# Down-projection of a decoder layer: seven block products in place of eight, with weight sums made in an earlier stage

## The chip, the cores and the metric

One core of one Trainium2 chip runs the whole layer. The metric is device time in microseconds (us). Before the change the median of three runs is 3149.24 us (3142.88 to 3153.28); the execution that was profiled took 3145.07 us. Engines are named as in the profile: PE (TensorE), PEld (its weight loads), DVE (VectorE), ACT (ScalarE), POOL (GpSimd), SP (SyncE, which issues nearly all DMAs, in order).

## The reference

One layer over 2048 tokens of width 1024, all in float32: a normalised and modulated input projection, two kinds of causal attention (8 stick-breaking heads, then 8 "FoX" heads with forget gates), an output projection, a gated MLP with a width-3 causal convolution, and a last RMS norm. What the change touches is the end of it:

```python
h = rms_norm(x, g_mlp[l]) * (1.0 + scale_m) + shift_m
u = causal_depthwise_conv(h @ w_up[l], conv_w[l], conv_b[l])
u_gate, u_val = jnp.split(u, 2, axis=-1)
x = x + gate_m * ((jax.nn.silu(u_gate) * u_val) @ w_down[l])
return rms_norm(x, g_final)
```

`w_down` is 2752 x 1024, so the inner dimension is 21 full blocks of 128 channels and one of 64. `gate_m` is one number for each of the 1024 output columns, made from the conditioning vector `c`.

## The kernel before

**Precision.** A float32 product is made of three matmuls of a reduced-precision type. `split` (L43) writes the high part of an operand on ACT (`AF.Copy`, L44) and the remainder on POOL or DVE (`tensor_sub`, L45); the three matmuls are high x high, high x low, low x high. L44 and L45 are thus the lines of every operand in the profile; the tile's name tells which.

**Stages.** The stick-breaking attention takes the first 950 us or so, the FoX attention about 950 to 1640, the output projection to about 1790, the up-projection with convolution to about 2660, the down-projection to the end. In the attention stages `units` (L579) are (kind, head pair, block of 512 tokens); while one unit attends, `interleave` (L137) advances "fillers" by a number of steps for each unit: the next unit's projection (`proj`, L347, which loads eight `hp` tiles by L352), and, in the FoX stage, `late_mod` (L528). That generator makes the four later parts of the modulation from `w_ada` (ACT L554, POOL L552 and L555); after part 2 it folds the attention gate into `w_out` (`fold_out`, L515: 16 operand tiles stored to DRAM by L525), and after part 5 it stores the MLP's gate as `gate_m` (L568). It gets 4 steps for each unit from the second FoX unit on (L694). All its tiles are `hp` tiles (`h_tile`, L182, ten buffers of 512 KB), which the projection uses too. POOL has further work there: a memset for each diagonal tile of attention weights (L399), and small squares (L483).

**The up-projection** (L811 to L926) is already done as seven block products for eight (Winograd's form of Strassen's method): for each block of 128 channels POOL makes four sums of the weights (L799, L800, L801, L805), seven operands are split, and seven products run. Its results, `silu(u_gate) * u_val` with channels on the partitions, are stored to the DRAM tiles `gs` (L904, L926).

**The down-projection** (L929 to L996). For each of four blocks of 512 tokens, all 22 channel blocks are gone through. `load` brings 128 channels of `w_down` (512 KB, `wdraw`) and of `gs` (256 KB, `graw`) and splits both. 8 PSUM banks hold 4 token tiles x 2 column halves; each gets three matmuls of 128x128 by 128x512 for a channel block (two for the half block, whose two parts share one tile). At the end of a token block each bank is multiplied by the gate (`gm`, L986), added to the residual `xo` (L987), squared and normalised (L989 to L995), and written out.

**Order.** A list scheduler orders each engine's instructions when the program is built; every engine then runs its own list in order. A tile gets a buffer when one of its name's is free, so that a load into a buffer waits on SP for that buffer's last reader, and what stands behind it on SP waits too.

## Time and profile before

| what | us |
|---|---|
| median of three runs | 3149.24 |
| profiled execution | 3145.07 |
| its span on the core | 3143.3 |
| PE busy in the span | 2990.1 |
| DVE / ACT / POOL busy | 2158.8 / 1652.0 / 1215.3 |
| first matmul of the down-projection | 2662.12 |

A line of the groups view reads: line, engine, operation, tiles written and read, shape, count, then busy time and mean duration (ns) of one, then idle time of the engine ahead of them and who ended it. A row of the view by stretches gives, for a stretch of the span, the busy time and count of each engine, the granted clock of PE (1 is full), the share of the 16 DMA engines that was busy, and GB/s. A row of the timeline gives start, length, engine, line, operation and count. The view of waits gives who waited for whom, total us, times, longest.

### The profile page before, as it was taken

To read this page: it belongs to the slowest core of one execution; us is meant where nothing else is said; L and a number is where in the kernel's file an instruction comes from. 1 tells how busy PE (TensorE), PEld (TensorE's weight loads), DVE (VectorE), ACT (ScalarE), POOL (GpSimd) and SP (SyncE) were. 2 spreads that over 40 slices of the span, in tenths; PEclk is the share of its full clock that TensorE was granted. 3 is DMA by queue.
4 is the path that set the end of the run, shared out by engine and by line. 5 is a ranking of instruction groups with operands and counts; after the bars stand their busy time and mean duration, and the time that the engine had idled before them with its cause. 6 is when DMAs were issued, how large, how long until landed. Compare 5 with 4: busy or idle time off the path is not lost.

```text
span 3143.3 us, 46642 instructions
## 1 busy us (share of the span) xinstructions
PE 2990.1 (95%) x16190; PEld 2521.1 (80%) x16190; DVE 2158.8 (69%) x3343; ACT 1652.0 (53%) x3033; POOL 1215.3 (39%) x1391
## 2 busy tenths in 40 slices
PE   6899998999989999999999999999899998999998
PEld 5778787877878889888877678888678887888887
DVE  6787888978866775556843587777987776254253
ACT  5565666656756665556744444444444444343332
POOL 2563555647543132142112344444444442322321
PEclk8999999999999999999999999999999999999999
DMA  9447542455336695685546632222222223554552
GB/s 267 167 156 247 169 128 78 159 200 161 127 107 225 204 306 184 188 298 177 170 154 219 213 101 81 86 87 82 84 80 83 88 86 123 195 199 161 190 199 90
DMA packets 292941, 496.53 MB, mean 158 GB/s; under 512 B 29449, under 2 KB 177665, under 8 KB 291681
## 3 DMA queue, kind: packets, MB, share of 16 engines
q1 hardware_dynamic: 281072, 480.92, 47.9%
q10 hardware_dynamic: 11632, 12.63, 1.1%
q8 instruction: 128, 2.10, 0.3%
q14 instruction: 109, 0.88, 0.1%
HBM read 352.61 MB, written 90.51 MB: 141 GB/s over the span
## 4 chain that ended last, share of the span: by engine, by line
PE 57%; DVE 13%; DMA 12%; POOL 7%; issue 6%; ACT 4%; SPq 1%; ACTq 0%; POOLq 0%; DVEq 0%
PE ps_pj L287 8%; PE ps_o L963 8%; PE ps_pv L405 6%; PE ps_o L813 6%; PE ps_pt L396 5%; PE ps_pj L326 5%; PE ps_t L963 4%; PE ps_bc L963 4%; DMA wuraw<-in_w_up_dram 3%; PE ps_qk L384 3%; PE ps_qk L385 3%; DVE r L426 2%; DVE wu L45 2%; PE ps_t L813 2%; DMA Q<-q 2%
## 5 line engine op out<-in xcount | busy, mean ns | idle before, releaser
L813 PE MATMUL ps_o<-oa,wu 128*128 128x512 f32 x2088 | 503.3, 392 | 12.6 <-DVE oa L45 7.5
L813 PEld LDWEIGHTS ps_o<-oa,wu 128*128 128x128 f32 x2088 | 390.7, 188 | 104.2 <-DVE oa L45 11.8
L405 PE MATMUL ps_pv<-at,V 128*128 128x256 f32 x2304 | 416.4, 299 | 25.6 <-DVE at L401 12.5
L401 DVE TENSOR_TENSOR at<-ps_pt,at 128x512 fp32r<-128x512 f32 (+1 forms) x576 | 363.4, 651 | 109.1 <-ACT at L400 106.5
L400 ACT ACTIVATE at<-ps_pt 128x512 fp32r<-128x512 f32 (+1 forms) x576 | 315.7, 577 | 209.6 <-PE ps_pt L396 165.8
L287 PE MATMUL ps_pj<-hp,w_qk 128*128 128x512 f32 x1512 | 414.1, 405 | 11.9 <-POOL hp L45 3.4
L426 DVE TENSOR_TENSOR_SCAN r<-r 128x513 f32<-128x513 f32 (+2 forms) x320 | 383.6, 1213 | 40.2 <-ACT r L419 30.5
L427 POOL TENSOR_TENSOR a<-a,r 128x512 f32<-128x512 f32 (+3 forms) x240 | 280.3, 1171 | 310.5 <-DVE r L426 178.9
L405 PEld LDWEIGHTS ps_pv<-at,V 128*128 128x128 f32 x2304 | 339.0, 194 | 61.5 <-DVE at L401 25.1
L287 PEld LDWEIGHTS ps_pj<-hp,w_qk 128*128 128x128 f32 x1512 | 273.4, 190 | 65.8 <-POOL hp L45 4.5
L45 DVE TENSOR_TENSOR wd<-wdraw,wd 128x1024 fp32r<-128x1024 f32 x88 | 112.2, 1275 | 260.9 <-ACT wd L44 260.8
L384 PE MATMUL ps_qk<-K,Q 128*128 128x512 f32 (+2 forms) x640 | 269.5, 421 | 12.0 <-DMA K<-q 6.2
L45 POOL TENSOR_TENSOR g<-graw,g 128x512 fp32r<-128x512 f32 x84 | 141.4, 1685 | 325.9 <-ACT g L44 325.8
L963 PE MATMUL ps_o<-wd,g 128*128 128x512 f32 x1040 | 250.2, 390 | 8.8 <-ACT g L44 8.8
L326 PE MATMUL ps_pj<-w_v,hp 128*128 128x256 f32 (+1 forms) x1536 | 241.1, 293 | 3.8 <-DVE q L296 2.0
L813 PE MATMUL ps_t<-ob,wu 128*128 128x512 f32 x984 | 241.6, 390 | 0.0
L385 PE MATMUL ps_qk<-K,Q 128*128 128x512 f32 (+2 forms) x640 | 238.5, 373 | 0.0
L963 PEld LDWEIGHTS ps_o<-wd,g 128*128 128x128 f32 x1040 | 195.6, 188 | 49.8 <-ACT g L44 9.2
L44 ACT ACTIVATE wu<-wuraw 128x512 fp32r<-128x512 f32 x214 | 133.2, 626 | 184.4 <-PE ps_o L813 114.7
L326 PEld LDWEIGHTS ps_pj<-w_v,hp 128*128 128x128 f32 x1536 | 212.5, 194 | 13.3 <-DVE q L296 2.8
L813 PEld LDWEIGHTS ps_t<-ob,wu 128*128 128x128 f32 x984 | 184.8, 188 | 39.1 <-DVE wu L45 0.3
L396 PE MATMUL ps_pt<-ident,a 128*128 128x128 f32 x1088 | 185.6, 280 | 21.7 <-POOL a L427 13.2
(221 smaller groups left out, 5665.2 us busy)
## 6 DMA issues: line engine op xcount, KB each, us to landing
hp<-hs SPq DMA_DIRECT2D x224, 512.0 KB
wuraw<-in_w_up_dram SPq DMA_DIRECT2D x84, 512.0 KB
wdraw<-in_w_down_dram SPq DMA_DIRECT2D x84, 512.0 KB
Q<-q SPq DMA_DIRECT2D x128, 256.0 KB
g<-u SPq DMA_DIRECT2D x42, 512.0 KB
graw<-g SPq DMA_DIRECT2D x84, 256.0 KB
hs<-hp SPq DMA_DIRECT2D x32, 512.0 KB
K<-q SPq DMA_DIRECT2D x128, 128.0 KB
```

What stands on the lines that cost most here:

```text
L45: (lo_engine or nc.gpsimd).tensor_sub(lo, src, f(hi))
L287: nc.tensor.matmul(acc, w[kt][:, a, n], h[:, bb], start=kt == 0 and i == 0, stop=kt == KT - 1 and i == 2)
L326: nc.tensor.matmul(av[:, t * width:(t + 1) * width], hts[kt][:, a, tok], w[1][kt][:, bb, 0:width], start=kt == 0 and m == 0, stop=kt == KT ...
L384: nc.tensor.matmul(b[:, :cw], Q[:, hl, 0, qcols], K[:, hl, :cw], start=True, stop=False)
L385: nc.tensor.matmul(b[:, :cw], Q[:, hl, 1, qcols], K[:, hl, :cw], start=False, stop=not last)
L396: nc.tensor.transpose(b[:, i * P:(i + 1) * P], blk(kts[kk], qi), ident)
L400: nc.scalar.activation(at[:, 0, lo:], b[:, lo:], AF.Copy)
L401: nc.vector.tensor_sub(at[:, 1, lo:], b[:, lo:], f(at[:, 0, lo:]))
L405: nc.tensor.matmul(o[:, 0:2 * P], V[kt // 4][:, kt % 4, hl, :], rhs, start=first and kk == 0 and w == 0, stop=last and kk == 1 and w == 1)
L426: nc.vector.tensor_tensor_scan(rev, rev, rev, 1.0, ALU.mult, ALU.bypass)
L813: nc.tensor.matmul(b, w[:, p, j], o[:, q], start=first and i == 0, stop=last and i == 2, skip_group_check=True)
L963: nc.tensor.matmul(banks[t][n], g[:, a, t * P:(t + 1) * P], w[:, b, n * TB:(n + 1) * TB], start=k == 0 and i == 0, stop=k == NKD - 1 and i ...
```

## The change

**The products.** The down-projection goes by pairs of token tiles (8 pairs `tp` of 2 x 128 tokens) and pairs of channel blocks (11 pairs `m`), against the two halves of the 1024 columns: a 2x2 by 2x2 block product, done with seven products of sums of blocks. The 64 channels of the last block are filled up to 128 with zeros. The 11 channel pairs are worked in three chunks of 4, 4 and 3 (`CHUNKS`); for each chunk all eight token pairs are gone through. A product is 12 matmuls in the first two chunks and 9 in the last. The loop's PSUM banks are `a`, `b` and `d`; the first product (`p1`) is copied by ACT and added by POOL to three of the four blocks of the residual, the others are added by DVE (`take`).

**The running sum.** A token pair's residual rows (`xo`, four buffers) are read from `x1s`, the chunk's products are added, and they are stored to `x1s` again; the last chunk normalises and writes the output.

**Weight operands.** A new filler `fold_down` in `late_mod` (in place of the store of `gate_m`) multiplies `w_down` by the gate and forms the seven weight operands for each channel pair, a quarter of the columns of both halves at a time: 22 times two loads, two multiplications, four sums on POOL and seven stores of 128 KB to the DRAM tiles `wds`. `late_mod` gets 7 steps for each unit in place of 4. In the down-projection `down_operand` loads one operand of a chunk (1 MB, or 768 KB) into one of two `wbraw` buffers and splits it (remainder on POOL for operands 5 and 6, on DVE for the others) into one of seven `wb` buffers.

**Token operands.** `g_operands` loads 8 (or 6) pieces of `gs` of 128 KB for a token pair, makes four sums on POOL, and splits seven operands (remainder on POOL for three, on DVE for four).

```diff
-    gate_m = dram.tile([P, D], F32, name="gate_m")
+    NM = (NFULL + 1) // 2
+    CHUNKS = [(m, min(4, NM - m)) for m in range(0, NM, 4)]
+    wds = [[dram.tile([P, n, TB], F32, name=f"wd{o}_{c}") for o in range(7)] for c, (_, n) in enumerate(CHUNKS)]
...
+    def fold_down(gt):
+        q4 = lambda x: x.rearrange("p (h q n) -> p q h n", h=2, n=2 * P)
+        for m, q in ((m, q) for m in range(NM) for q in range(2)):
+            t = wide().rearrange("p (w n) -> p w n", n=2 * P)
...
+            for i, rows_ in ((0, P), (1, n)):
+                row = (2 * m + i) * P
+                nc.sync.dma_start(t[0:rows_, 2 * i:2 * i + 2], q4(w_down[row:row + rows_, :])[:, q])
+                nc.gpsimd.tensor_mul(t[:, 2 * i:2 * i + 2], t[:, 2 * i:2 * i + 2], q4(gt)[:, q])
+            yield
+            a1, a2, b1, b2 = (t[:, i] for i in range(4))
+            to = [w[:, m % 4, q * 2 * P:(q + 1) * 2 * P] for w in wds[m // 4]]
+            for o, x in ((0, a1), (2, b1), (5, b2)):
+                nc.sync.dma_start(to[o], x)
+            nc.gpsimd.tensor_sub(b2, b2, a2)
+            nc.gpsimd.tensor_sub(a2, a2, a1)
+            nc.gpsimd.tensor_add(a1, b2, a1)
+            nc.gpsimd.tensor_sub(b1, b1, a1)
+            for o, x in ((4, b2), (3, a2), (1, a1), (6, b1)):
+                nc.sync.dma_start(to[o], x)
+            yield
...
-                    nc.sync.dma_start(gate_m, gt)
+                    yield from fold_down(gt)
...
-                    (lm if kind == "fox" and (p, tb) != (0, 0) else None, 4, False), (tail, 12, True)])
+                    (lm if kind == "fox" and (p, tb) != (0, 0) else None, 7, False), (tail, 12, True)])
...
+    def down_operand(c, o):
+        n = CHUNKS[c][1]
+        w = dp.tile([P, 2, 4, TB], F32R, name="wb", bufs=7)
+        raw = dp.tile([P, 4, TB], F32, name="wbraw", bufs=2)
+        nc.sync.dma_start(raw[:, 0:n], wds[c][o])
+        split(w[:, 0, 0:n], w[:, 1, 0:n], raw[:, 0:n], nc.gpsimd if o > 4 else nc.vector)
+        return w
+
+    def g_operands(c, tp):
...
+        raw = dp.tile([P, 2, 4, 2 * P], F32, name="graw", bufs=2)
...
+        s2, s3 = (dp.tile([P, 4, P], F32, name="gsum", bufs=3)[:, 0:n] for _ in range(2))
+        def put(x, engine=None):
+            g = dp.tile([P, 2, 4, P], F32R, name="ga", bufs=8)
+            split(g[:, 0, 0:n], g[:, 1, 0:n], x, engine or nc.vector)
+            return g
+        nc.gpsimd.tensor_sub(s3, a11, a21)
+        nc.gpsimd.tensor_add(a21, a21, a22)
+        nc.gpsimd.tensor_sub(s2, a21, a11)
+        yield put(a11)
+        yield put(s2)
+        yield put(a12)
+        nc.gpsimd.tensor_sub(a12, a12, s2)
+        yield put(a21)
+        yield put(s3, nc.gpsimd)
+        yield put(a12, nc.gpsimd)
+        yield put(a22, nc.gpsimd)
...
+        a = bank_a()
+        run(a, 0, True, True)
+        p1 = de.tile([P, TB], F32, name="p1", bufs=2)
+        nc.scalar.activation(p1, a, AF.Copy)
+        for t, half in ((1, L), (1, H), (0, H)):
+            nc.gpsimd.tensor_add(xs[t][:, half], xs[t][:, half], p1)
+        b = bank_a()
+        run(b, 1, True, True)
+        take(1, L, b)
+        run(a, 2, False, True)
+        take(0, L, a)
+        square(0, L)
+        run(b, 3, False, True)
+        take(1, H, b)
+        d = bank_c()
+        run(d, 4, True, True)
+        take(1, H, d)
+        square(1, H)
+        run(b, 5, False, True)
+        take(0, H, b)
+        square(0, H)
+        norm(0)
+        run(d, 6, False, True)
+        take(1, L, d)
+        square(1, L)
+        norm(1)
```

`run` issues the matmuls of one product, then the next token pair's operand (`next(nxt)`) and, in the last pair of a chunk, the next chunk's weight operand; `square` and the scaling in `norm` act in the last chunk alone, before that `norm` stores the rows to `x1s`.

More of the change, by code (lines that the diff above doesn't have):

```diff
@@ new lines, with run, take, square @@
+    L, H = slice(0, TB), slice(TB, D)
+    order = [(c, tp) for c in range(len(CHUNKS)) for tp in range(S // (2 * P))]
+    gen = g_operands(*order[0])
+    wbs, ga = [], []
+    for o in range(7):
+        wbs.append(down_operand(0, o))
+        ga.append(next(gen))
+    for i, (c, tp) in enumerate(order):
+        n = CHUNKS[c][1]
+        nxt = g_operands(*order[i + 1]) if i + 1 < len(order) else None
+        turn = nxt is not None and order[i + 1][0] != c
+        final = c == len(CHUNKS) - 1
+        xs = [de.tile([P, D], F32, name="xo", bufs=4) for _ in range(2)]
+        for t in range(2):
+            nc.sync.dma_start(xs[t], x1s[2 * tp + t])
+        later, wlater = [], []
+        def run(b, o, first, last):
+            for m in range(n):
+                for k, (p, q) in enumerate(((0, 0), (0, 1), (1, 0))):
+                    nc.tensor.matmul(b, ga[o][:, p, m], wbs[o][:, q, m], start=first and m == 0 and k == 0,
+                                     stop=last and m == n - 1 and k == 2, skip_group_check=True)
+            if nxt is not None:
+                later.append(next(nxt))
+            if turn:
+                wlater.append(down_operand(c + 1, o))
+        def take(t, half, b):
+            nc.vector.tensor_add(xs[t][:, half], b, xs[t][:, half])
+        ss = de.tile([P, 4], F32, name="sl_f", bufs=4)
+        def square(t, half):
+            if final:
+                junk = de.tile([P, TB], BF16, name="junk_f", bufs=2)
+                k = 2 * t + (half is H)
+                nc.scalar.activation(junk, xs[t][:, half], AF.Square, accum_out=ss[:, k:k + 1])
+        def norm(t):
+            row = 2 * tp + t
+            if not final:
+                nc.sync.dma_start(x1s[row], xs[t])
+                return
+            r = de.tile([P, 1], F32, name="r_f", bufs=4)
+            nc.vector.tensor_add(r, ss[:, 2 * t:2 * t + 1], ss[:, 2 * t + 1:2 * t + 2])
```

78 lines of the change are left out of this document (20 added, 58 removed).

## The prediction

> **What bounds the kernel now.** First the page's busy times and the chain that ended last: they say which engine to count on.
>
> ```profile
> span 3143.3 us, 46642 instructions
> PE 2990.1 (95%) x16190; PEld 2521.1 (80%) x16190; DVE 2158.8 (69%) x3343; ACT 1652.0 (53%) x3033; POOL 1215.3 (39%) x1391
> PE   6899998999989999999999999999899998999998
> PE 57%; DVE 13%; DMA 12%; POOL 7%; issue 6%; ACT 4%; SPq 1%; ACTq 0%; POOLq 0%; DVEq 0%
> ```
>
> PE is the bound nearly everywhere. Then the two stages that the change touches, by stretches (busy us and count of PE, PEld, DVE, ACT, POOL; clock; DMA share; GB/s), and PE's waits in each: FoX first, then the end.
>
> ```profile
> 950.00:1150.00 200.00, 199.12 (x1307) 173.31 (x1306) 142.30 (x363) 129.17 (x246) 52.73 (x71) 1.00 0.72 240
> 1150.00:1450.00 300.00, 294.67 (x1963) 263.50 (x1962) 177.12 (x448) 175.94 (x316) 90.43 (x100) 0.99 0.73 233
> 2662.00:2674.00 12.00, 11.88 (x46) 9.79 (x47) 4.45 (x4) 4.48 (x7) 4.13 (x3) 0.87 1.03 406
> 2700.00:3100.00 400.00, 400.00 (x1767) 331.20 (x1766) 155.57 (x173) 139.37 (x211) 122.01 (x73) 1.00 0.54 179
> ...
> PE ps_pt L396 <- ACT p L455: 3.8, 3, 2.5
> ...
> PE ps_o L963 <- ACT g L44: 8.8, 1, 8.8
> ```
>
> From 2700 to 3100 PE never pauses and its clock is full: 400/1767 = 0.2264 us for a matmul. The only wait of the down-projection is 8.8 us at its start. FoX is as full (493.8 of 500 us), and its longest kind of wait sums to 3.8 us. So a matmul less is worth 0.2264 us in the last stage, and whatever makes PE late in FoX is paid in full.
>
> **The matmuls removed.** Before: 4 token blocks x (21 x 24 + 16) = 2080, as the groups say. After: 7 products x 8 token pairs x 3 x (4 + 4 + 3) = 1848.
>
> ```profile
> L963 PE MATMUL ps_o<-wd,g 128*128 128x512 f32 x1040 | 250.2, 390 | 8.8 <-ACT g L44 8.8
> L963 PE MATMUL ps_bc<-wd,g 128*128 128x512 f32 x520 | 131.3, 389 | 0.0
> L963 PE MATMUL ps_t<-wd,g 128*128 128x512 f32 x520 | 131.3, 390 | 0.0
> ```
>
> 232 x 0.2264 = **52.5 us saved**. (An eighth would be 260; the zero-filled half block costs the rest.) A product of 12 takes 2.72 us, a pair of seven 19.0 us, in the last chunk 14.3.
>
> **The start of the stage.** The timeline of SP, ACT and PE around the present start:
>
> ```profile
> 2653.35 0.78 SPq L956 DMA_DIRECT2D gf<-in_g_final_dram  x1
> 2654.23 0.44 SPq L938 DMA_DIRECT2D wdraw<-in_w_down_dram  x1
> 2656.94 3.87 SPq L978 DMA_DIRECT2D xo<-x1s  x4
> 2661.44 0.48 SPq L926 DMA_DIRECT2D g<-u  x1
> ...
> 2654.23 6.24 DMA wdraw<-in_w_down_dram
> ...
> 2660.49 1.06 ACT L44 ACTIVATE wd<-wdraw 128x1024 fp32r<-128x1024 f32 x1 [1.34 <-DMA wdraw<-in_w_down_dram]
> 2662.12 2.08 PE L963 MATMUL ps_o<-wd,g 128*128 128x512 f32 x4 [8.80 <-ACT g L44]
> ```
>
> Today the first weights are issued at 2654.23, ahead of the last store of `g` (2661.44, which waits for DVE). In the changed program's order on SP, `gf`, four `xo` and that store come first, and then the first `wbraw`, eight `graw`, the second `wbraw`, eight more `graw`, the third. So the first operand is issued 7 us later, lands at about 2667 (1 MB at the 406 GB/s above is 2.6 us, plus a fixed part: the 512 KB took 6.24 with others ahead), and needs its split:
>
> ```profile
> L44 ACT ACTIVATE wd<-wdraw 128x1024 fp32r<-128x1024 f32 x88 | 93.1, 1058 | 211.3 <-PE ps_bc L963 197.9 <-DMA wdraw<-in_w_down_dram 13.4
> L45 DVE TENSOR_TENSOR wd<-wdraw,wd 128x1024 fp32r<-128x1024 f32 x88 | 112.2, 1275 | 260.9 <-ACT wd L44 260.8
> L45 POOL TENSOR_TENSOR g<-graw,g 128x512 fp32r<-128x512 f32 x84 | 141.4, 1685 | 325.9 <-ACT g L44 325.8
> ```
>
> For 128x2048 that is about 1.9 us on ACT (estimated with the 128x512 rows below), 2 x 1.275 = 2.5 on DVE, 4 x 1.685 = 6.7 on POOL. Two staging buffers serve seven operands: 5 us to land, 1.9 and 2.5 to be split, then the buffer's next load; two operands per 9.4 us, one per 4.7, where a product is 2.72. The seventh lands at 2667 + 3 x 9.4 = 2695, some 5 later for 2 MB of `graw` between, and its remainder is ready 8.6 after: 2709. PE's order puts twelve products of the first three token pairs ahead of it, so that at 2712 thirteen products (35.3 us) are done: the stage stands as if it had begun at 2676.5 instead of 2662.1. I take **+15**; bounds: 10 (the first operand's lateness alone) and 30 (as if nothing were pulled ahead).
>
> **The two turns between chunks.** The same ring refills seven operands, but the first two are prefetched, and PE's order leaves ten to eleven products between the last use of an old operand and the first use of the new one. By the 4.7 us, operand 6 is ready some 42 us after the old pair began and is used at about 42. Nothing to spare: **+5** for both; bounds 0 and 30 (each like the start).
>
> **The steady state.** Per token pair POOL has four sums, three remainders and three additions to `xo`: ten 128x512 operations, in the last chunk seven of 128x384 and three of 128x512. The trace has that operation at very different prices:
>
> ```profile
> L555 POOL TENSOR_TENSOR hp<-hp 128x512 f32<-128x512 f32 x51 | 64.8, 1293 | 74.0 <-ACT hp L554 73.9
> L805 POOL TENSOR_TENSOR wuraw<-wuraw,ws 128x512 f32<-128x512 f32 x42 | 87.5, 2083 | 95.4 <-DVE wu L45 95.3
> L45 DVE TENSOR_TENSOR wu<-ws,wu 128x512 fp32r<-128x512 f32 x82 | 60.6, 739 | 107.7 <-ACT wu L44 107.5
> L867 DVE TENSOR_TENSOR y<-ps_o,snap 128x512 f32<-128x512 f32 x40 | 27.4, 686 | 13.6 <-PE ps_o L813 11.9
> L44 ACT ACTIVATE g<-graw 128x512 fp32r<-128x512 f32 x84 | 51.9, 618 | 33.9 <-DMA graw<-g 33.8
> ```
>
> At 1293 ns a pair is 12.9 us of 19.0, at 1685 16.9, at 2083 20.8. DVE per pair has four remainders of 739 and seven additions of 686: 7.8 us. The dear POOL rows stand beside DVE work on two SBUF tiles, the cheap one beside DVE work from PSUM; here only 3 of 19 us are of the first kind, so I take about 1.35 us: 13.5 of 19.0, and about 11.2 of 14.3 in the last chunk. ACT has 7 x 0.618 and a copy, 4.9 us. The running sum adds 1 MB in and 1 MB out to 1 MB of `graw`: 165 GB/s where 179 flow today. All of it hides behind PE, whose order runs two or three products between a product and the one that needs its bank back. **+3** for late hand-overs; bounds 0 and 53 (rival C).
>
> **The fold in FoX.** 44 loads and 154 stores, 31.5 MB, and 44 x 1.29 + 88 x 0.7 (0.755 in the 128x256 row, with its 512 twin at 1.293) = 118 us of POOL. The 44 of 105 filler steps spread them over 6.3 of 16 units, some 270 us: +117 GB/s on 233, and POOL from 30% to 74%, waits not counted. These are the rows for and against cover:
>
> ```profile
> 1075.00:1100.00 25.00, 24.66 (x160) 21.20 (x158) 14.10 (x36) 14.24 (x32) 5.64 (x7) 1.00 1.01 332
> 1525.00:1550.00 25.00, 24.94 (x167) 21.86 (x166) 18.74 (x47) 16.04 (x30) 5.33 (x9) 1.00 1.01 366
> 1250.00:1275.00 25.00, 21.11 (x135) 19.15 (x134) 10.00 (x24) 10.55 (x21) 2.80 (x3) 0.86 0.98 281
> ...
> POOL at L399 <- PE ps_pv L405: 183.9, 34, 19.7
> ...
> L45 POOL TENSOR_TENSOR hp<-hp 128x512 fp32r<-128x512 f32 x16 | 20.5, 1291 | 30.6 <-ACT hp L44 21.1 <-DMA wos<-hp 7.2 <-DMA K<-q 2.3
> L617 POOL TENSOR_TENSOR o<-o,r 128x256 f32<-128x256 f32 x22 | 16.5, 755 | 39.3 <-DMA o<-os 24.7 <-DMA r<-rstd 7.3 <-DVE at L401 3.0
> L399 POOL MEMSET at<- 128x256 f32 x60 | 18.7, 312 | 205.8 <-PE ps_pv L405 183.9 <-PE ps_pt L396 6.5 <-DVE at L401 5.9
> ```
>
> Twice the DMA engines were full for 25 us and PE lost nothing; once it lost 4 us beside them. The first subtraction of a step overwrites what a store is reading, so POOL waits for that store (such a wait on `wos` took 7.2 us), with the attention's memsets behind it; on SP the projection's `hp` loads stand behind stores that wait for POOL, and the opening burst holds five of ten `hp` buffers. In the changed order about one memset falls to a fold step of some 12 us, in which the step's POOL work is 5.4 us and a wait. I take **+8**: two stalls like that of 1250. Bounds 0 and 63 (rival B).
>
> **The tail.** One multiplication of DVE less behind the last matmul, **-0.7**.
>
> **The sum.** -52.5 + 15 + 5 + 3 + 8 - 0.7 = -22.2 us. On the profiled execution: 3145.07 - 22.2 = 3122.9. The median of the runs lies 4.2 above that execution, so a median should be about **3127 us**, 0.7% less.
>
> **Rivals.**
>
> A, the forecast: 3127; with all small bounds 3106 to 3140.
>
> B, slower: **the fold stands on POOL ahead of the memsets.** Some 25 memsets fall into the stretch; a transposition and its copy cover about 2 us of delay. If half of them sit behind a store wait of 7 us, PE loses 12.5 x 5 = 63 in place of 8: 3182. It decides once a memset loses over 1.2 us beyond its cover, for 25 of these eat the other 30 us of gain. For: the one measured wait on a store, and a queue in order. Against: POOL already stands 184 us at those memsets, so it usually gets there first.
>
> C, slower: **POOL becomes the last stage's bound.** At 2083 ns a pair takes 20.8 us against 19.0 and about 17.3 against 14.3: 16 x 1.8 + 8 x 3.0 = 53 in place of 3: 3177. It decides above 1.9 us per operation. Against: the DVE mix above.
>
> D, little change: **the weight ring paces the start and both turns.** 30 for the start and 10 for the turns in place of 20 give 3147.
>
> E: **DVE's two-tile operations stop POOL for their whole length.** Added to 1.293 each, four remainders of 0.739 make a pair 15.9 us, still hidden; in the last chunk, about 10.8 plus four remainders of about 0.55 and four scalings of 0.845 make 16.4 against 14.3, and 8 x 2.1 less the 3 is +14: 3141. The Trainium skill, "SBUF — State Buffer", section "SBUF: two separate sides", calls the port pair that DVE (with two SBUF inputs) and GpSimd share an exclusive lock, not a division of bandwidth. By that rule E is the case; the 1293, 1685 and 2083 ns above agree in kind.
>
> ```profile
> L995 DVE SCALAR_TENSOR_TENSOR xo<-xo,r_f,gf 128x512 f32<-128x512 f32 x32 | 25.7, 845 | 0.3
> ```
>
> That fewer products don't run is excluded: the built program holds 1848 matmuls.
>
> **Chances.** A 0.50, B 0.17, C 0.10, D 0.15, E 0.08. About 0.3% (9.4 us) is what a measurement of this kernel can tell from no change: 3139.8 to 3158.7 is the same. Faster is A and half of E's mass and spread, 0.55; the same is D and the rest, 0.18; slower is B and C, 0.27. The range 3106 to 3178 holds A, D, E, most of C and B's milder half and leaves out under 0.2; the forecast's own range is 3106 to 3140.
>
> **What would show it.** Right: 1848 matmuls at 0.226 us; PE busy over 98% in the steady stretches of the last stage; one gap of 15 to 20 us at its start with small waits on `wb`; FoX ending within 10 us of now. Wrong: PE waits on `hp` or `at` in FoX that sum to over 30 us (B); POOL over 90% busy in the last stage with `xo` or `ga` as PE's releaser (C, E); waits for `wbraw` at each turn (D).

## The result, and the profile after the change

The changed kernel takes 3193.77 us (median of four runs, 3187.51 to 3198.42), the kernel before, on the same chip, 3146.65 (four runs, 3142.88 to 3153.28). The ratio is 1.0145 with a 95% interval of 1.0127 to 1.0162: **slower by about 47 us**, where 22 us less were forecast, and above the range. The profiled execution took 3198.42 us.

The lines of the page that answer to those shown of before:

```profile
span 3196.6 us, 47300 instructions
PE 2975.7 (93%) x15958; PEld 2499.5 (78%) x15958; DVE 2263.3 (71%) x3442; ACT 1655.6 (52%) x3070; POOL 1572.4 (49%) x1695
PE   6899998999989999899999999999899998899997
PE 22%; DVE 7%; DMA 7%; POOL 6%; issue 3%; ACT 1%; SPq 1%; POOLq 0%; DVEq 0%; ACTq 0%
```

PE is busy 14 us less, and the span is 53 us longer. (The shares of the chain add up to 47% here: it reaches back over half the span only, so it says nothing of FoX.) The same stretches as before, and those of the last stage, which now runs from 2701 to the end (columns as in the rows of before):

```profile
950.00:1150.00 200.00, 191.51 (x1229) 165.93 (x1228) 138.33 (x337) 130.50 (x245) 76.18 (x86) 0.99 0.84 288
1150.00:1450.00 300.00, 278.48 (x1815) 247.08 (x1814) 169.70 (x428) 145.17 (x267) 137.60 (x176) 0.95 0.72 226
2700.00:2720.00 20.00, 1.32 (x6) 0.75 (x4) 5.98 (x6) 4.72 (x4) 0.47 (x1) 0.64 0.85 295
2720.00:2770.00 50.00, 41.73 (x149) 31.68 (x150) 30.59 (x23) 20.76 (x24) 48.43 (x24) 0.84 0.61 218
2770.00:2870.00 100.00, 100.00 (x443) 82.80 (x442) 45.59 (x55) 29.12 (x47) 81.12 (x59) 1.00 0.54 182
2870.00:2970.00 100.00, 94.54 (x410) 77.53 (x409) 57.48 (x55) 33.77 (x46) 81.20 (x49) 0.98 0.66 225
2970.00:3070.00 100.00, 97.85 (x425) 80.46 (x424) 52.24 (x57) 34.99 (x54) 75.91 (x56) 0.98 0.55 188
3070.00:3190.00 120.00, 103.90 (x428) 80.96 (x426) 88.00 (x126) 47.31 (x122) 80.31 (x69) 0.97 0.42 144
```

PE's waits (total us, times, longest): in FoX (900 to 1700) of before, then of the changed kernel, then in its last stage.

```profile
PE ps_pj L287 <- DMA hp<-hs: 2.2, 2, 1.7
```

```profile
PE ps_pj L289 <- DMA hp<-hs: 22.1, 10, 4.1
...
PE ps_pv L407 <- POOL at L401: 2.2, 2, 1.8
```

```profile
PE ps_o L1021 <- DVE xo L1029: 20.7, 13, 5.1
PE ps_o L1021 <- ACT ga L44: 19.5, 2, 18.8
PE ps_o L1021 <- DVE wb L45: 4.4, 3, 3.5
```

Two places carry the result. **FoX**: its last weighted sum comes at 1648.5 instead of 1604.9, 43.6 us later. In the two stretches of FoX PE was busy 493.8 of 500 us before and is 470.0 now, and in the second the mean matmul is longer too (278.48/1815 = 153.4 ns for 294.67/1963 = 150.1; the mix of shapes has a share in that), at a granted clock of 0.95 for 0.99. PE's wait for the projection's `hp` tiles is ten times what it was (22.1 us for 2.2), and its wait for POOL's memsets is 2.2 us in all.

The waits alone don't make up 43.6 us. The clock adds to them: between 950 and 1650 PE ran at a granted clock of 0.50 for 34 us in seven pieces, and for 6.8 us in one piece before, which by an estimate from these lengths is some 14 us of work lost. Five of the seven begin within a wait for `hp` of over 2 us or just behind it, as this one does at a wait of 3.85 us that ends at 1405.6:

```profile
1405.00:1412.00 7.00, 6.36 (x19) 5.08 (x20) 1.62 (x5) 1.67 (x2) 1.15 (x3) 0.52 1.04 390
```

With the 20 us of added waits for `hp` that makes 34 of the 43.6; the rest is smaller waits.

**The last stage**: it lasts 495.3 us for 490.0 though it holds 232 matmuls less. The 1848 at 0.2264 us and 8 us behind the last one are 426, so 69 us are lost in it, 11 before. They lie at the start (a gap of 18.84 us for 8.8, then 149 matmuls in 50 us where 221 would fit and the kernel before ran 214: some 25 us more than in the kernel before), at the turns (410 and 425 matmuls in 100 us for 443: 7 and 4 us), and in the last chunk (428 matmuls in 118 us: some 22 us). Between, from 2770 to 2870, nothing is lost.

### The profile page after: what moved, and what is told of

Its sections match the earlier page's. It is cut to its first block, busy times and chain, and to the rows that moved or that the text cites. A ratio compares the mean times of both kernels' runs of the same rounds, so it can differ in the third digit from the quotient of the medians.

```text
span 3196.6 us, 47300 instructions
## 1 busy us (share of the span) xinstructions
PE 2975.7 (93%) x15958; PEld 2499.5 (78%) x15958; DVE 2263.3 (71%) x3442; ACT 1655.6 (52%) x3070; POOL 1572.4 (49%) x1695
## 5 line engine op out<-in xcount | busy, mean ns | idle before, releaser
L289 PE MATMUL ps_pj<-hp,w_qk 128*128 128x512 f32 x1512 | 426.9, 413 | 31.9 <-DMA hp<-hs 22.1
L1021 PE MATMUL ps_o<-wb,ga 128*128 128x512 f32 x1320 | 326.4, 402 | 46.7 <-DVE xo L1029 20.7
L1021 PEld LDWEIGHTS ps_o<-wb,ga 128*128 128x128 f32 x1320 | 254.6, 194 | 109.2 <-ACT ga L44 26.1
L421 ACT ACTIVATE r<-ps_qk 128x512 f32<-128x512 f32 (+2 forms) x320 | 172.9, 541 | 62.2 <-PE ps_qk L387 36.1
L45 DVE TENSOR_TENSOR wu<-wuraw,wu 128x512 fp32r<-128x512 f32 x214 | 185.1, 868 | 12.8 <-ACT wu L44 12.8
```

The lines of the kernel that those rows point to most:

```text
L45: (lo_engine or nc.gpsimd).tensor_sub(lo, src, f(hi))
L289: nc.tensor.matmul(acc, w[kt][:, a, n], h[:, bb], start=kt == 0 and i == 0, stop=kt == KT - 1 and i == 2)
L1021: nc.tensor.matmul(b, ga[o][:, p, m], wbs[o][:, q, m], start=first and m == 0 and k == 0, stop=last and m == n - 1 and k == 2, skip_group_ ...
```

## The experiments

Two theories of FoX. **Theory 1**: the loads of `hp` come late, because the fold and the denser filler put transfers, bytes and held buffers in their way. **Theory 2**, the prediction's rival B: the fold's POOL work and its waits stand ahead of the memsets of the attention. For the last stage: the start and turns are paced by the weight ring, or POOL is the bound, or DVE hands `xo` over late. Ratios below are against the kernel before; 0.001 is 3.15 us, and a ratio's interval is some 0.0015 to each side, so that a difference of two has about 7 us of doubt.

**e1: seven steps of filler, and nothing else.** Before, with `4` as `7` in the line of `interleave`.

```diff
-                    (lm if kind == "fox" and (p, tb) != (0, 0) else None, 4, False), (tail, 12, True)])
+                    (lm if kind == "fox" and (p, tb) != (0, 0) else None, 7, False), (tail, 12, True)])
```

> The kernel before with the later modulation's filler at 7 steps for each unit instead of 4, and nothing else. Theory: in the changed kernel's FoX stage the projection's hp loads come late (PE waited 22 us for them, and lost more at a lower clock), and most of that is the fold itself; then this costs 3 to 12 us, since the changed kernel lost some 8 us between 1025 and 1100, before the fold began. Rival: the denser filler alone makes the transfers collide; then most of the 46 us by which the FoX stage grew shows here: +30 to +46.

Measured: 1.0042 (1.0027 to 1.0057), 13 us. PE's waits in FoX:

```profile
PE ps_pj L287 <- DMA hp<-hs: 6.5, 4, 2.9
```

The modulation's own loads of `w_ada`, pushed closer together, make the projection's loads late. From 1040 to 1140 the DMA share is 0.95 for 0.84, and PE is busy 90.9 us for 99.3. The waits on `hp`, 6.5 us for 2.2, show only a part of the 13 us. The prediction had no term for this.

**e2: the fold alone.** Before, with the seven steps and `fold_down`; `gate_m` and the down-projection of before stay, and no operand is used.

```diff
                     nc.sync.dma_start(gate_m, gt)
+                    yield from fold_down(gt)
```

> The kernel before with the fold added in the FoX stage (7 steps for each unit) and its down-projection left as it was; the folded weights are stored and not used. Theory: the loss in FoX and the loss in the last stage are separate and add; then this is 46 us (40 to 52) slower than before, all of it between the first FoX logits and the last weighted sum. Rival: the FoX stage was longer only because later stages pull on it (buffers, order): then under +25.

Measured: 1.0144 (1.0125 to 1.0163), 45 us, and the last weighted sum at 1651.5. All of FoX's loss is there with the fold and its steps alone. PE, SP and POOL in FoX, from the same kernel's waits:

```profile
PE ps_pj L290 <- DMA hp<-hs: 26.1, 13, 5.4
```

```profile
SPq L547 <- POOL hp L542: 34.6, 23, 3.8
...
SPq L553 <- POOL hp L548: 19.3, 15, 3.1
```

```profile
POOL hp L542 <- DMA hp<-in_w_down_dram: 72.0, 13, 9.2
...
POOL hp L548 <- DMA wd<-hp: 45.9, 15, 6.6
```

POOL does stand in the fold's waits for 118 us, as rival B said. What waits for it is hardly PE (4.0 us at the memsets) but SP: its stores stand 54 us for POOL's products and sums, in the queue in which the `hp` loads stand too.

**e3: the down-projection alone.** The change's last stage, with four steps and no fold. The operands are read from stretches of `w_down`, so this kernel leaves out the gate and the sums of the weights; e10, e13 and e14 do so too.

```diff
-                    yield from fold_down(gt)
+                    nc.sync.dma_start(gate_m, gt)
...
-        nc.sync.dma_start(raw[:, 0:n], wds[c][o])
+        k = 4 * c + o
+        flat = w_down[0:2 * (DFF // 2), :].rearrange("(r a) n -> r (a n)", a=2)
+        nc.sync.dma_start(raw[:, 0:n].rearrange("p a n -> p (a n)"), flat[k % 10 * P:(k % 10 + 1) * P, 0:n * TB])
```

> The changed down-projection with nothing folded: 4 steps, no fold, and the seven weight operands of a chunk are read from stretches of w_down of the same size and layout, so that the output is not the reference's (the gate and the weight sums are left out, all transfers, splits and matmuls of the last stage are there). Theory: the last stage loses at its start (26 us beyond the present one), its turns (11) and in the last chunk (22) what 232 matmuls fewer save (52.5), so that this stands within 10 us of before: -5 to +10. Rival: the last stage only looks slow because the earlier disturbance moved its start against DVE's last work on g; then 30 us or more faster than before.

Measured: 1.0018 (1.0008 to 1.0028), 6 us slower. Seven products for eight give nothing back even when the sums are free. With e2 this makes 51 us; the whole change is 46 by its ratio: within the doubt, the parts add up.

**e5: the fold without POOL.** As e2, without the two products and four sums of a step; the loads and stores remain.

```diff
-                nc.gpsimd.tensor_mul(t[:, 2 * i:2 * i + 2], t[:, 2 * i:2 * i + 2], q4(gt)[:, q])
...
-            nc.gpsimd.tensor_sub(b2, b2, a2)
-            nc.gpsimd.tensor_sub(a2, a2, a1)
-            nc.gpsimd.tensor_add(a1, b2, a1)
-            nc.gpsimd.tensor_sub(b1, b1, a1)
```

> As the fold alone (the kernel before's down-projection), but the fold's six POOL operations for each step are left out: it loads w_down and stores the same 154 pieces, unscaled and unsummed. Theory: the transfers, their place on SP's queue and the hp buffers that they hold make the hp loads late: at least 25 of the 46 us remain. Rival, as the prediction's case B had it: the fold's work on POOL, ahead of the attention's memsets, is what costs; then under +15 is left.

Measured: 1.0142 (1.0119 to 1.0166), 45 us: the same within some 8 us. Theory 2 falls: PE hardly waits at POOL's memsets (2.2 us in the changed kernel, 4.0 in e2), and without POOL's work the time stays.

The stores that wait for POOL are not cleared by this. In the changed kernel the three longest waits on `hp` (4.1, 3.9 and 3.9 us, 11.9 of the 22.1) begin at the end of these stretches, in which the DMA engines were far from full (0.36, 0.32 and 0.49; e2 has the same):

```profile
1283.00:1293.00 10.00, 8.09 (x49) 6.79 (x47) 4.38 (x14) 4.38 (x14) 3.43 (x6) 0.83 0.36 119
1339.00:1349.00 10.00, 9.69 (x79) 9.19 (x77) 4.78 (x13) 4.09 (x9) 4.62 (x6) 1.00 0.32 105
1392.00:1402.00 10.00, 9.79 (x76) 9.05 (x74) 7.11 (x18) 5.90 (x13) 4.90 (x6) 1.00 0.49 156
```

SP issued the loads of `hp` late there, behind stores of the fold that stood for POOL and loads of the fold that stood for stores:

```profile
1285.60 2.74 SPq L552 DMA_DIRECT2D wd<-hp  x4
1290.03 1.21 SPq L540 DMA_DIRECT2D hp<-in_w_down_dram  x2
1291.34 3.48 SPq L354 DMA_DIRECT2D hp<-hs  x5
...
1297.05 1.22 PE L289 MATMUL ps_pj<-hp,w_qk 128*128 128x512 f32 x2 [4.12 <-DMA hp<-hs]
```

In e5 the transfers come denser (a DMA share of 0.87 from 1135 to 1480, 0.76 in e2), and its waits on `hp` come beside fuller engines (0.88 and 1.02 in the 10 us ahead of two of the longest). One way of being late has taken the place of another, at the same price.

**e9: the fold's transfers thin.** As e5, with 16 of 128 partitions in each load and store.

```diff
-                nc.sync.dma_start(t[0:rows_, 2 * i:2 * i + 2], q4(w_down[row:row + rows_, :])[:, q])
+                nc.sync.dma_start(t[0:16, 2 * i:2 * i + 2], q4(w_down[row:row + 16, :])[:, q])
...
-                nc.sync.dma_start(to[o], x)
+                nc.sync.dma_start(to[o][0:16], x[0:16])
```

> As the fold without its POOL work, with every load and store cut to 16 of 128 partitions: the same number of DMAs in the same kind of order on SP, the same hp buffers held, an eighth of the bytes (the fold's values are left out; nothing uses them). Theory, bytes: the DMA engines are nearly full in FoX and 31.5 MB more push the hp loads back; then this falls to the denser filler's 13 us above before, at most 20. Rival, queue and buffers: the hp loads stand behind the fold's DMAs on SP and the fold holds hp buffers; then 30 or more of the 45 us stay.

Measured: 1.0089 (1.0074 to 1.0104), 28 us. Seven eighths of the bytes are worth 17 of the 45, with some 9 us of doubt. The packets fall with the bytes (on the queue from 960 to 1640, 59,400 for 85,700 in e2), and a buffer is held for less time, so the three are not told apart.

**e8: few of them.** As e9, with one load and one store for each piece of the fold (two steps) where e9 has nine transfers; the `hp` buffer is taken and released as before.

```diff
-            for i, rows_ in ((0, P), (1, n)):
+            for i, rows_ in ((1, n),):
...
-            for o, x in ((0, a1), (2, b1), (5, b2)):
-                nc.sync.dma_start(to[o][0:16], x[0:16])
...
-            for o, x in ((4, b2), (3, a2), (1, a1), (6, b1)):
+            for o, x in ((6, b1),):
```

> The thin fold (no POOL work, 16 of 128 partitions per transfer), which cost 28 us with all its transfers, now with one load and one store a step in place of two loads and three or four stores; the hp buffers are taken and released as before. It leaves out the fold's values. Theory 1, what is left beside the denser filler's 13 is the number of transfers on SP's queue: the cost falls to about 16 to 18. Theory 2, it is the hp buffers that a step holds while its load comes: the cost stays at 25 to 28, and PE's waits on hp at about 12 us.

Measured: 1.0066 (1.0049 to 1.0082), 21 us: between the two expectations. PE's waits on `hp` go down from run to run, from 26.1 (e2) over 17.7 (e5) and 12.0 (e9) to 8.1 us here. With e1 at 13, some 8 us are left for a held buffer and two thin transfers a piece, some 7 for the other seven transfers; each has about 7 us of doubt, so neither stands clear of it.

**e7: another queue.** As e2, with the fold's loads and stores issued by ACT (`nc.scalar.dma_start`).

> The down-projection as before, the fold in FoX with seven steps, but its loads and stores issued on ACT's queue; no operand is used. With them on SP's queue it cost about 45 us. Theory 1, the projection's hp loads are late because they stand behind the fold's issues on SP's queue (its stores waited 33.6 us there for POOL in the changed kernel): the hp waits of PE fall to those of the denser filler alone (6.5 us) and the cost to about 13 to 25. Theory 2, the lateness comes from the hp buffers that the fold holds and from the bytes: about 45 again, with hp waits of 18 to 26 us. Theory 3, the queue in order matters wherever it is: stores that wait for POOL now stand before ACT's exponentials, the attention waits for those, and the cost is 60 or more.

Measured: 1.0148 (1.0131 to 1.0165), 47 us. The `hp` waits halve to 12.9 us and the time stays; ACT now stands 12.3 us at a tile of attention weights (`at`) for the fold's stores, and on SP the projection's loads stand 65 us for `hp` buffers that the fold still holds (36.2 us for its stores, 28.9 for its loads). So SP's order is a part of the way in which FoX loses the time, and with another issuing engine others take its place. Which of them did, the load on the transfers or the shared buffers, is not told apart: no run in FoX gave the fold buffers of its own.

**e10: the first product's additions by DVE.** As e3, without `p1`: no copy by ACT, and `take` adds the bank to three quarters of `xo`.

```diff
-        p1 = de.tile([P, TB], F32, name="p1", bufs=2)
-        nc.scalar.activation(p1, a, AF.Copy)
         for t, half in ((1, L), (1, H), (0, H)):
-            nc.gpsimd.tensor_add(xs[t][:, half], xs[t][:, half], p1)
+            take(t, half, a)
```

> The changed down-projection alone (weights read from w_down, nothing folded), with the three additions of the first product made by DVE from PSUM instead of by ACT's copy and POOL. Theory: in the last stage DVE's additions, and PE behind them, wait for POOL's additions (35 us) and DVE's own two-tile operations are stretched by POOL (1218 ns where 739 stand in the up-projection); with POOL at seven operations of ten the last stage gets 8 to 20 us shorter than in the run with the down-projection alone, some 5 to 15 us faster than before. Rival: the wait is for the residual's load from DRAM and the ring of four xo buffers, whoever adds: within 5 us of that run; and as DVE then has 77 more operations, it may be later by 5.

Measured: 0.9999 (0.9988 to 1.0009), 6 us less than e3. The groups of DVE by form, of the changed kernel and of e10:

```profile
L1029 DVE TENSOR_TENSOR xo<-ps_o,xo 128x512 f32<-128x512 f32 x96 | 65.4, 686 | 124.9 <-PE ps_o L1021 80.7 <-POOL xo L1057 35.5 <-DMA xo<-x1s 4.2
L45 DVE TENSOR_TENSOR ga<-graw,ga 128x512 fp32r<-128x512 f32 x48 | 58.3, 1218 | 14.0 <-ACT ga L44 14.0
```

```profile
L1032 DVE TENSOR_TENSOR xo<-ps_o,xo 128x512 f32<-128x512 f32 x168 | 110.1, 684 | 132.7 <-PE ps_o L1024 79.8 <-DMA xo<-x1s 44.8 <-PE ps_t L1024 7.9
L45 DVE TENSOR_TENSOR ga<-graw,ga 128x512 fp32r<-128x512 f32 x48 | 51.7, 1080 | 1.6 <-ACT ga L44 1.5
```

DVE's additions waited 35.5 us for POOL's; without those the wait moves to the load of `xo` (44.8 for 4.2 us), which on SP waits for stores from `xo`. Most of the lateness of `xo` was covered by that next wait.

**e13: chunks of 3, 4, 4.** As e10, with the short pairs first, and the last store of `g` issued by ACT.

```diff
-    CHUNKS = [(m, min(4, NM - m)) for m in range(0, NM, 4)]
+    CHUNKS = [(0, 3), (3, 4), (7, 4)]
...
-        nc.sync.dma_start(gs[NFULL][sblk], sg[REST:P])
+        (nc.scalar if sblk else nc.sync).dma_start(gs[NFULL][sblk], sg[REST:P])
```

> The changed down stage alone (weights read from w_down, so the gate and the weight sums are left out), the first product's three additions by DVE from PSUM, chunks of 3, 4, 4 channel pairs in place of 4, 4, 3, and the last store of g issued on ACT's queue. The version with chunks 4, 4, 3 was level with before. Theory 1, the start is set by what must land and be split for the first ring, and the last chunk by what must be done per pair in 14.3 us: a first chunk a quarter smaller starts the matmuls 3 to 5 us earlier, and a last chunk with 19 us a pair loses some 10 us less; 3133 to 3142, ratio 0.994 to 0.998. Rival: the short pairs now stand first, where the weight ring is also filling, and lose there what the end gains: level, 0.999 to 1.002.

Measured: 0.9962 (0.9947 to 0.9976), 12 us faster than before. The gap at the start falls from 19.6 us (e10) to 15.1, of which the store of `g` has some 3, as f1 and f2 below put it (19.8 and 16.6), so the shorter first chunk gives some 1.5 there. The stretch at the end is now close to full. Of e10, then of e13:

```profile
3060.00:3130.00 70.00, 59.27 (x239) 46.16 (x238) 51.64 (x79) 25.00 (x66) 27.85 (x27) 0.95 0.43 141
```

```profile
3060.00:3130.00 70.00, 65.24 (x287) 53.42 (x285) 46.56 (x75) 23.61 (x57) 22.74 (x17) 1.00 0.36 120
```

A pair of nine matmuls a product leaves DVE 14.3 us for its additions, norms and remainders; with twelve it has 19.0, and PE's waits on `xo` in the last 120 us of the span fall from 16.6 us (e10) to 3.6. That is most of what the last chunk lost.

**e14: g in fewer transfers.** As e13, with `g` stored in one DRAM tile for each chunk and half, so that a pair's six or eight loads become two.

> As the version with chunks of 3, 4, 4, and g stored so that the eight loads of graw for a token pair become two transfers. The eight took SP 7.6 us to issue in the changed kernel, before the second weight operand could be issued. Theory 1, the issue of the many small loads delays the first operands: the first matmul comes 4 to 6 us earlier and the next 50 us lose less, 5 to 10 us in all against the chunks of 3, 4, 4. Rival: the start is paced by bytes and by the splits on ACT and DVE: no more than 2 us are won.

Measured: 0.9965 (0.9952 to 0.9978): level with e13, a miss. SP issued the first eight loads of the changed kernel in 7.63 us (0.95 us each, with 128 KB), but with two transfers in their place the gap at the start is 14.98 us for 15.10.

```profile
2709.02 0.53 SPq L965 DMA_DIRECT2D wbraw<-wd  x1
2709.65 7.63 SPq L979 DMA_DIRECT2D graw<-g  x8
2717.33 0.43 SPq L965 DMA_DIRECT2D wbraw<-wd  x1
...
2720.16 0.79 PE L1021 MATMUL ps_o<-wb,ga 128*128 128x512 f32 x1 [18.84 <-ACT ga L44]
```

(These rows of the timeline are of the changed kernel: SP's issues ahead of the first product.)

**The fold elsewhere.** Five kernels tried the up-projection, where 85 GB/s flow and POOL is busy 42%. **f1** is the whole change with `fold_down` advanced once for each channel block there, in one buffer of its own; **f2** is f1 with the last store of `g` on ACT.

> The changed kernel with the fold moved out of FoX: 4 steps as before, gate_m stored and loaded, and the fold's steps taken in the up-projection, one for each channel block, with a buffer of its own. There the DMA engines are busy 0.26 to 0.3 and POOL 0.43. Theory: FoX is back at before's length, the up-projection takes the fold for 0 to 8 us, and what is left is the last stage's own balance (+5.7 without the fold): 0 to +14 us against before. Rival: DVE, busy 0.78 there with two-tile operations, is held up by POOL and becomes the up-projection's bound: +20 or more.

> As the fold in the up-projection, and the last store of g is issued on ACT's queue, so that the first weight operand's load no longer stands behind it on SP (it waited there from 2704 to 2708.4, and PE stood idle for 18.8 us). Theory: the start of the last stage is 4 to 6 us earlier, all of which shows. Rival: the load waits for its buffer anyway, or ACT's own work behind the store is held up: within 2 us of the run with the fold in the up-projection.

Measured: 1.0296 (1.0281 to 1.0312) and 1.0282 (1.0267 to 1.0297). The up-projection, full before, ends some 90 us later in f1. What the store on ACT gives is within the doubt: 4 ± 7 us in the time, though the gap at the start is 3 us shorter. The same stretch of before, then of f1:

```profile
1900.00:2200.00 300.00, 299.18 (x1313) 245.76 (x1313) 235.25 (x270) 132.20 (x188) 125.99 (x124) 1.00 0.28 85
```

```profile
1900.00:2200.00 300.00, 257.85 (x1029) 203.15 (x1030) 203.38 (x212) 102.71 (x148) 208.26 (x200) 0.93 0.47 146
```

POOL's sums of the up-projection's weights stand there behind products that wait 65.8 us for the fold's loads.

**g1** takes that wait away: 44 pieces of a quarter of the columns, loaded a slot ahead into two buffers, sums into a tile of their own, with the last stage of e13. **g2** is g1 with the grouped `g` of e14.

```diff
+            t = up_.tile([P, 2, 2, P], F32, name="ft", bufs=2)
...
+            fs_ = up_.tile([P, 4, P], F32, name="fsum", bufs=1)
+            nc.gpsimd.tensor_sub(s4, b2, a2)
+            nc.gpsimd.tensor_sub(s3, a2, a1)
+            nc.gpsimd.tensor_add(s1, s4, a1)
+            nc.gpsimd.tensor_sub(s6, b1, s1)
```

> The whole change with all its parts computed, rearranged after the runs so far: chunks of 3, 4, 4, the first product's additions by DVE from PSUM, the last store of g on ACT's queue, and the fold out of FoX (four steps of filler, as before) into the up-projection, in 44 pieces of a quarter of the columns with buffers of their own: each piece is loaded a slot (about 20 us) ahead, its sums go to a tile of their own, and its stores are issued in the middle of the slot, so that neither POOL nor SP stands waiting for the fold. The same down stage without any fold was 0.9962 of before. Theory 1, the fold is dear where its transfers and stores stand in front of work that PE waits for, not for its operations: here it costs 0 to 10 us, 3137 to 3147, ratio 0.996 to 0.999. Rival, POOL's 118 us and the added traffic cost PE time wherever they are, because POOL and DVE slow one another in the up-projection: 15 to 40 us, ratio 1.001 to 1.009.

> As the version with the prefetched fold, and g stored so that a token pair's eight loads become two. Without a fold this grouping was worth nothing beside the chunks of 3, 4, 4 (0.9965 and 0.9962). Theory: the same within 0.15%. Rival: with more transfers on SP's queue at the end of the up-projection fewer issues start the last stage earlier, 3 to 6 us.

Measured: 1.0196 (1.0182 to 1.0211) and 1.0233 (1.0216 to 1.0250), misses both; why g2 is 12 us behind g1 nothing here explains. The list scheduler put all 44 pieces into the first half of the up-projection, because nothing held them back:

```profile
1900.00:2000.00 100.00, 85.64 (x342) 66.74 (x341) 63.08 (x69) 35.08 (x51) 83.25 (x111) 0.93 0.53 156
2000.00:2100.00 100.00, 87.11 (x348) 67.41 (x347) 66.95 (x73) 35.24 (x51) 89.68 (x114) 0.93 0.55 159
...
2400.00:2500.00 100.00, 100.00 (x442) 82.41 (x441) 78.48 (x90) 44.62 (x62) 43.00 (x32) 1.00 0.30 87
```

**g3** spreads them, by a one-element copy on DVE that makes each load wait for its block's `y`.

```diff
+            if pace:
+                nc.vector.tensor_copy(t[0:1, :, 0, 0:1], pace[-1][0:1, 2:4].rearrange("p (a b) -> p a b", b=1))
```

> As the version with the prefetched fold, but a one-element copy of DVE makes each piece's load wait for the y tile of its slot: in that version the scheduler had put all 44 pieces into the first half of the up-projection (POOL 76 to 90% busy there, PE 83 to 87%) and lost some 65 to 75 us. Now one piece falls into each of the 42 slots, behind the weight sums. Theory 1, what cost time there was POOL, pushed to 76 to 90% with the fold's operations between the weight sums; at some 57 to 63% and behind the sums the fold costs 0 to 15 us: 3137 to 3152, ratio 0.996 to 1.001. Rival, every operation of the fold lengthens the DVE and POOL work beside it and PE pays in proportion, whatever the density: 40 us or more, ratio 1.009 or more.

Measured: 1.0364 (1.0342 to 1.0385), the worst of all. POOL is at 53 to 58% throughout, and PE at 86 to 92%:

```profile
PE ps_o L816 <- DVE snap L865: 76.1, 32, 4.3
```

So POOL's density was not the cause, or not the only one. The copies take DVE 30 us of a queue in which the additions that free PE's banks stand, and the weight loads stand on SP behind the fold's loads, which wait 418 us for DVE's copies. Which of these, or POOL's work itself, costs the time is not told apart: what the fold would cost in the up-projection with no such side effect stays open.

**The parts put together.** **h2** is the whole change with the fold left in FoX at seven steps, its seven stores merged into two (three raw quarters, then four sums), and the last stage of e13. **h1** is h2 with one step of filler for a piece and six steps a unit.

```diff
-            for o, x in ((0, a1), (2, b1), (5, b2)):
-                nc.sync.dma_start(to[o], x)
+            nc.sync.dma_start(to[:, 0:3], t[:, 0:3])
...
-            for o, x in ((4, b2), (3, a2), (1, a1), (6, b1)):
-                nc.sync.dma_start(to[o], x)
+            nc.sync.dma_start(to[:, 3:7], t)
```

> The whole change, fold in FoX with seven steps as changed, but a fold step's seven stores are merged into two (the three raw quarters, then the four sums), and the down stage has chunks of 3, 4, 4, the first product's additions by DVE and the last store of g on ACT's queue. By the parts so far: 45 of the fold, less 14 of the rearranged down stage, less some 5 to 9 for the fewer transfers (cutting a thin step to one load and one store had saved 9): 22 to 26 us slower than before, ratio 1.007 to 1.009. Rival, the number of transfers matters only where they are thin, since full ones are paced by bytes: 31, ratio 1.010.

> As the version with merged stores, but the fold takes one step of filler in place of two and FoX's units get six steps each in place of seven. Theory, the denser filler (13 us from four to seven steps) shrinks with the steps: 3 to 5 us less, ratio 1.005 to 1.008. Rival, a step that does a load, its products and its stores at once crowds the queues more than it saves: no gain or a loss.

Measured: h2 1.0064 (1.0047 to 1.0081), 20 us slower than before, and h1 1.0086 (1.0073 to 1.0099), 27. For h2 the parts say 45 - 12 = 33, so the merged stores are worth some 13 us, with all their bytes and some 9 us of doubt (the sum takes three runs to be additive); PE's waits on `hp` in FoX fall to 12.1 us. h1 brings no gain over h2 (7 us more, with as much doubt), as its rival said, though its `hp` waits are 25.7 us: a load and its stores in one step may crowd the queue more than six steps relieve it, which no run shows. h2 is the fastest complete form of the change that was found, some 25 us ahead of the changed kernel; no form that makes the sums beat the kernel before.

## Why the prediction was wrong, point by point

**The matmuls, -52.5: right.** 1848 of them, and 443 in 100 us in the undisturbed stretch, 0.2257 us each.

**The fold in FoX, +8: wrong, and the largest miss.** It cost 45 (e2). The step that failed is "two stalls like that of 1250". It took cover for each operation by itself: DMA engines full for 25 us without loss, POOL idle at the memsets. In its place the runs show PE waiting 22.1 us for `hp` loads and running 34 us at half the clock.

Rival B's sign, waits on `hp` or `at` of over 30 us, was all but met by another mechanism: the waits were for loads, hardly for memsets, and without POOL's work the cost stayed (e5). So that sign could not tell the two apart. What the prediction named but did not price is its half sentence on SP, that the projection's `hp` loads stand behind stores that wait for POOL. In the changed kernel that was at work in 11.9 of the 22.1 us.

By the experiments the 45 are about 13 for the denser filler (e1), 17 for bytes and packets (e2 to e9), and 15 for the number of transfers and the buffers held (e9 to e1), of which e8 and h2 put some 7 to 13 on the number; each difference has 7 to 9 us of doubt. How a load comes late (its place in the queue, a burst, a buffer) stays open in part. The row of 1150 to 1450 gives a warning by an estimate: 233 GB/s at a DMA share of 0.73, so that 117 GB/s more ask for 1.10 of the engines. That is not what came: the fold's transfers took from 1135.5 to 1478.6, 343 us for the 270 assumed, at 226 GB/s and a share of 0.72 in the same stretch. From 950 to 1150, nearly all of it ahead of the fold's first load, the share rose to 0.84 and PE lost 7.6 us.

**The start, +15: right in kind, too small, and within its bounds of 10 to 30.** It cost some 25. The first matmul comes 18.84 us after the last of the up-projection, ten more than before; then 149 matmuls run in 50 us, at a granted clock of 0.84. The forecast counted the first operand's lateness and then let PE's order hide the ring; the first operands come one by one, and PE stops at each. The first matmuls take 0.79 and 0.80 us, where the group's mean is 0.402 and the steady ones take 0.389. The Trainium skill, "TensorE: Matmul & The Clock Gate", section "Part 1: The HAM clock gate (the "warmup" mystery)", says that the idle state runs at half the clock until some 3.4 us of activity have passed; the rows agree with the half. In the trace the clock is at 0.50 until 2725.9 and twice more, from 2729.3 to 2732.7 and from 2736.2 to 2743.0.

**The two turns, +5: low, within the bounds of 0 and 30.** 7 and 4 us.

**The steady state, +3: wrong at one end.** Nothing is lost from 2770 to 2870, with POOL at 81%. The last chunk lost some 22 us: not by POOL's rate (67% there, 80.31 of 120 us) as in rivals C and E, but in the main by the hand-over of `xo`, where DVE waits for POOL and POOL for the load. Of the 20.7 us of PE's waits on it 13.1 lie in this chunk; the 428 matmuls took 0.243 us each in place of 0.2257, some 7 us more, at a clock of 0.97. e10 and e13 took most of it away by DVE additions and by keeping the short pairs off the end. (DVE has six additions a pair, not the seven that the prediction counted, since POOL has the other three: 7.1 us for 7.8, which changes nothing.)

**E's mechanism** is there, on the other side from where it was put. The Trainium skill, "SBUF — State Buffer", section "SBUF: two separate sides", has DVE (with two SBUF inputs) and GpSimd hold the shared ports one at a time. By form, DVE's remainder of 128x512 took 739 ns in the up-projection before and takes 1218 here beside a POOL that is busy 81%; the additions from PSUM stay at 686. POOL's own operations of that shape take 1386 to 1575 ns, near the 1.35 us that were chosen. So the rule agrees in kind, and DVE bore the price. With less POOL work (e10) it is 1080.

**The tail, -0.7:** hardly a difference, 8.0 us from the last matmul to the end before and 7.8 now.

**The sum.** The last stage was put at -30.2 (-52.5 + 15 + 5 + 3 - 0.7), and measures +5.3; FoX was put at +8, and ends 43.6 later. The fold is the largest single term, and the last stage's terms together missed as much (35.5 us). The output projection and the up-projection add 4.4, which nothing here explains.

## What to carry to other kernels

Price a stage's added transfers against its DMA share as a whole, not each against a stretch in which the engines were once full: where loads feed PE just in time, more bytes (some 17 us here) and more transfers (some 7 to 13) make PE wait, and a wait can lower its clock as well. Count what stands ahead of the critical loads in their queue. An engine's idle time is not cover as long as its work is tied to loads and stores that share a queue and buffers with the critical loads: SP's stores stood 54 us for POOL in e2. When fewer matmuls are bought with sums, run the stage with the sums left out first (e3 here, in one run): it says at once how much there is to spend, and here that was nothing until the chunks were rearranged, and 12 us then.

## What the runs showed of the hardware that had not been expected

- Without its POOL work the fold cost the same within some 8 us (1.0144 and 1.0142), though POOL's busy share in FoX went from 39% to 24%.
- A denser order of loads that were there before costs by itself: 13 us from four to seven steps.
- Merging seven stores of 128 KB into two was worth some 13 us with the bytes unchanged and some 9 us of doubt; issuing the fold's transfers from another engine gave nothing that shows (1.0144 and 1.0148).
- POOL's subtraction of 128x2048 took 4.70 us in the changed last stage, DVE's of the same shape 2.64.
- PE's clock halves without PE being idle. It stands at half for 3.4 us or a multiple of that. After the first 100 us of before, all 17 halvings followed 3.4 us in which PE was busy half of the time or less (mostly 0.35 to 0.50), and no such stretch with over half lost the clock; in the changed kernel the line lay at 0.53. In e2 stretches with 0.42 kept it and one with 0.67 lost it, so no exact line is shown.
